# A decoder layer with expert retrieval on one core: the gate table read one chunk later, one gather of V rows per chunk of U, two list rows in the output tile, list places by fewer sums

## The chip, the core and the metric

The kernel runs on one of the eight cores of a Trainium2 chip. The metric is the device time of one execution in microseconds (us). Five engines work side by side, each through its own queue in order: TensorE (PE in the profile, PEld for its weight loads), VectorE (DVE), ScalarE (ACT), GpSimd (POOL) and SyncE (SP). SP and POOL mostly issue transfers here; all transfers run on the core's 16 DMA engines. [...]

## What is computed

One layer of a decoder on 256 tokens of width 2048: attention of two kinds, attention into a memory, and then retrieval of experts (PEER), which takes the second half of the time. Only that last part is touched:

```python
s = jnp.einsum('thpd,hpkd->thpk', q, sub_keys)          # 8 heads, 2 x 128 keys
top_s, top_i = lax.top_k(s, 16)
cand = top_s[:, :, 0, :, None] + top_s[:, :, 1, None, :]
best_s, best_c = lax.top_k(cand.reshape(T, 8, 256), 16)
expert = ia * 128 + ib                                   # one of 16384
gate = jax.nn.softmax(best_s, axis=-1)
...
a = jnp.einsum('td,ted->te', xb, u_tab[eb])
hidden = gb * jax.nn.gelu(a)
out = jnp.einsum('te,ted->td', hidden, v_tab[eb])
...
y = rmsnorm(h + out)
```

So each of the 256 tokens picks 8 x 16 experts; each expert is one row of U and one of V, 2048 numbers each.

## The kernel before, in words

Products are made in float32 by splitting: a raw tile of 128x1024 is loaded (SP, line 68), ACT rounds it to `hi` (line 77), DVE makes `lo` = raw - hi (line 79), and PE multiplies both parts (lines 133 and 135). There are four `raw` buffers, three `hi` and three `lo`.

**The U stretch.** All 16384 rows of U are multiplied with all 256 tokens, in 128 chunks of 128 experts. One chunk is two raw tiles, 1 MB in all. Its result lands in one of 16 tiles `hb` (eight chunks each; the first eight tiles lie in pool `ba`, the rest in `bb`), where GELU is applied. For the gates, 256 indirect transfers (`put_gate`, line 1119) scatter the gate numbers into a table in DRAM, three or four per chunk, until chunk 66. The table is then read back, four chunks' worth per transfer: for chunks 0 to 79 into a tile `gates` out of the `raw` buffers, one read per chunk of U from chunk `end` (68) on, and DVE multiplies it into `hb` (line 841) a chunk later; for chunks 80 to 127 straight into `hb` ahead of the chunk.

**The lists.** `counts` notes for each expert how many tokens of each half (0 to 127, 128 to 255) use it. `lists` then gives each expert a place in one of five lists: one token of half 0, one token of half 1, few tokens of half 0, few of half 1, and everything else. Part 0 covers chunks 0 to 83, part 1 chunks 84 to 127. The steps `flags`, `totals`, `ranks`, `offsets`, `place` and `spots` (lines 929 to 990) are some 40 small DVE instructions and a few PE ones, and their last product is `where`, the places. After that POOL writes one indirect transfer per chunk (line 996): 84 for part 0 during the U stretch, 44 for part 1 during the V stretch.

**The V stretch.** The lists are cut into 88 sets of 128 experts, ordered in bundles by `plan`. For each set POOL gathers 128 rows of V (`fetch`, line 1173, 1 MB) into a freed `hb` tile, and SP loads the set's hidden numbers (`begin`, line 1222, 128 KB, the tile `listed`, a `raw` buffer). A `few` or `all` set needs `hh` and `hl` of its list rows (lines 1209 and 1211) and three products per half of the row, a `one` set two. The bundles 0 to 4 hold six sets that concern tokens 0 to 127 alone. They run while the seven steps of part 1's lists stand between them on DVE and PE. Ten sets are gathered ahead: one per chunk of U from the moment part 0's writes are all issued, and two per chunk at chunks 123 and 124 (`behind` ties each to the `lo` of a half chunk). From the V stretch on, gathers run 12 and later 16 sets ahead, and every second half set POOL issues one of part 1's 44 writes between them.

The order of instructions on each engine is made by a list scheduler from the program text; waits follow from the tiles that instructions read and write.

`fin`, the 128 x 4 x 2048 output tile, takes the space of the pair tile that the products of U read; its last quarter `fin[:, 3]` is first written when the first half of the output is normalised, at the end.

Of the kernel before, what the change touches and what calls it, by code (L numbers as in the profile page):

```python
# [18 lines left out]
F32 = mybir.dt.float32  # L19
F32R = mybir.dt.float32r  # L20
U32 = mybir.dt.uint32
# [4 lines left out]
ALU = mybir.AluOpType  # L26
# [27 lines left out]
class Layer:  # L54
# [663 lines left out]
    def peer(self):  # L718
        nc, tc, a = self.nc, self.tc, self.a
        with ExitStack() as es:  # L720
# [3 lines left out]
            self.total = [ba.tile([128, 128], F32, name="total%d" % tb) for tb in range(2)]  # L724
            self.place = [ba.tile([128, 128], U32, name="place%d" % tb) for tb in range(2)]
# [28 lines left out]
            with ExitStack() as e2:  # L754
# [66 lines left out]
                early = list(range(0, first, 4))  # L821
                done = {}
                part = 0
                late, steps = [], []
                while c < 128:
# [23 lines left out]
                    for k in range(2 if c > 123 else 1):  # L849
                        if part == 1 and not late and len(self.sets) < 10:  # L850
                            self.fetch(len(self.sets))
                            self.behind(self.gather, 2 - k)
# [4 lines left out]
                assert part == 1 and len(self.sets) == 10 and not late and not puts, (c, late, self.sets)  # L857
# [53 lines left out]
    def lists(self, part, pool, tag, bufs):  # L911
# [13 lines left out]
        q, m = self.total[0][:, :n], self.total[1][:, :n]  # L925
# [35 lines left out]
        def offsets():  # L961
            room = self.rooms[:, part * 4:part * 4 + 4]
            rest, spot = small[:, 0:4], small[:, 4:9]
            self.pin(v.tensor_add(rest, got["sum"][:, :4], room))
            v.tensor_copy(spot[:, 0:1], got["sum"][:, 4:5])
            v.tensor_scalar_max(rest, rest, 0.0)
            for j in range(4):
                v.tensor_add(spot[:, j + 1:j + 2], spot[:, j:j + 1], rest[:, j:j + 1])
            v.tensor_scalar(self.over[:, part:part + 1], spot[:, 4:5], -limit, 0.0, op0=ALU.add, op1=ALU.max)
            self.hold = v.tensor_add(spot[:, :4], spot[:, :4], room)  # L970

        def place():
            p = got["p"]
            self.pin(v.tensor_mul(q, p[:, 4, :], f[:, 4]))
            for j in range(4):
                v.scalar_tensor_tensor(ok[:, j], p[:, j, :], float(cap[j] * 128), f[:, j], op0=ALU.is_lt, op1=ALU.mult)
            v.tensor_sub(f[:, :4], f[:, :4], ok)
            for j in range(4):
                v.scalar_tensor_tensor(m, p[:, j, :], small[:, 4 + j:5 + j], f[:, j], op0=ALU.add, op1=ALU.mult)
                v.tensor_add(q, q, m)  # L980
            v.tensor_reduce(out=m, in_=f.rearrange("p k e -> p e k"), axis=AX.X, op=ALU.add)
            for j in range(4):
                self.hold = v.scalar_tensor_tensor(ok[:, j], p[:, j, :], float(base[j] - BIG), ok[:, j], op0=ALU.add, op1=ALU.mult)

        def spots():
# [3 lines left out]
            v.tensor_reduce(out=q, in_=ok.rearrange("p k e -> p e k"), axis=AX.X, op=ALU.add)  # L989
            self.hold = v.scalar_tensor_tensor(where, q, float(BIG), x, op0=ALU.add, op1=ALU.add)  # L990
# [188 lines left out]
    def v_phase(self):  # L1179
# [6 lines left out]
        with ExitStack() as es:  # L1186
# [67 lines left out]
            def run(upto, beside=[], steps=[], every=2):  # L1254


                while at[0] < self.ends[upto]:
# [8 lines left out]
                    for hf in range(2):  # L1266
                        for unit in units:
# [5 lines left out]
                            if turn[0] % every:  # L1273
                                continue
                            if steps:
                                steps.pop(0)()
                            elif beside:
# [250 lines left out]
```

## Time and profile before

| what | value |
|---|---|
| three runs | 1677.89, 1681.62, 1684.51 us (median 1681.62) |
| the profiled execution | 1684.47 us, of which the span 1682.7 |
| TensorE busy | 1620.0 us (96%), 8760 matmuls |
| VectorE, ScalarE, GpSimd busy | 75%, 60%, 44% of the span |
| moved | 418.82 MB, 249 GB/s over the span |
| U stretch | to about 1361 us; V stretch after it |

A window row gives, for a stretch of time, the busy us of each engine with the number of its instructions in brackets, then the granted TensorE clock (1.00 is full), the mean busy share of the 16 DMA engines and the GB/s moved. A timeline row gives start, duration, engine, line, operation, tiles, count, and in square brackets how long the engine stood idle before it and whom it waited for. Since TensorE's busy time is modelled, the number of matmuls in a window says more than its busy share: with nothing late, some 58 to 59 of the U stretch's fall into 10 us.

### The profile page before, as it was taken

How to read it: one execution, taken by the hardware profiler on the slowest of the kernel's cores; microseconds unless marked ns; L12 is line 12 of the kernel's file. 1: busy time of each engine (PE TensorE's matmuls, PEld its weight loads, DVE VectorE, ACT ScalarE, POOL GpSimd, SP SyncE). 2: the span in 40 equal slices, each digit the busy share in tenths (PEclk: the TensorE clock that was granted, in tenths of full speed). 3: DMA queues.
4: the chain of work that ended last, by engine and by line, in shares of the span. 5: the costliest groups of instructions: out<-in, count | busy, mean ns of one | idle time of the engine just before them, and what ended most of it. 6: DMA issues, size and time to landing. Idle time of an engine off the chain costs nothing. (4 is left out here: it accounts for less than half of the span.)

```text
span 1682.7 us, 25655 instructions
## 1 busy us (share of the span) xinstructions
PE 1620.0 (96%) x8760; PEld 1376.6 (82%) x8760; DVE 1262.5 (75%) x2265; ACT 1001.5 (60%) x1486; POOL 748.3 (44%) x656
## 2 busy tenths in 40 slices
PE   8999999999999999999999999999999979989996
PEld 6878777888889888888888878878888858767884
DVE  6876575555668998999999648878665578868687
ACT  6645556775566656666656436665555457656576
POOL 5420000211305266667788761102776318887630
PEclk9999999999999999999999999999999999999998
DMA  8768435789956756666656648876998958998991
GB/s 291 240 200 285 132 119 180 285 319 355 353 179 217 254 178 188 181 188 187 184 178 191 192 150 278 301 258 226 276 271 260 366 191 337 393 372 307 420 411 65
DMA packets 119884, 418.82 MB, mean 249 GB/s; under 512 B 22713, under 2 KB 34633, under 8 KB 106048
## 3 DMA queue, kind: packets, MB, share of 16 engines
q1 hardware_dynamic: 79632, 252.41, 46.5%
q0 software_dynamic: 39824, 164.16, 26.4%
q8 instruction: 70, 1.15, 0.3%
q14 instruction: 70, 0.57, 0.1%
q10 hardware_dynamic: 288, 0.52, 0.1%
HBM read 373.16 MB, written 51.75 MB: 253 GB/s over the span
## 5 line engine op out<-in xcount | busy, mean ns | idle before, releaser
L79 DVE TENSOR_TENSOR lo<-raw,hi 128x1024 fp32r<-128x1024 f32 x437 | 541.2, 1243 | 210.7 <-ACT hi L77 189.5
L77 ACT ACTIVATE hi<-raw 128x1024 fp32r<-128x1024 f32 x437 | 459.4, 1055 | 358.9 <-issue 145.7
L133 PE MATMUL acc<-pair_f,hi 128*128 128x512 f32 x2288 | 576.8, 394 | 6.1 <-ACT hi L77 6.1
L133 PEld LDWEIGHTS acc<-pair_f,hi 128*128 128x128 f32 x2288 | 412.4, 189 | 82.1 <-ACT hi L77 7.9
L1119 POOL DMA_INDIRECT table<-total,place x256 | 312.0, 1219 | 139.7 <-DVE lo L79 63.3
L135 PEld LDWEIGHTS acc<-pair_f,lo 128*128 128x128 f32 x2288 | 311.6, 191 | 30.8 <-DVE lo L79 9.3
L135 PE MATMUL acc<-pair_f,lo 128*128 128x256 f32 x2288 | 320.3, 283 | 7.0 <-DVE lo L79 7.0
L996 POOL DMA_INDIRECT rows<-hb,where x128 | 155.8, 1217 | 47.2 <-issue 28.9
L1173 POOL DMA_INDIRECT vrows<-V,index x88 | 125.9, 1430 | 112.2 <-issue 38.4
L115 DVE SCALAR_TENSOR_TENSOR lo<-vrows,val,hi 128x1024 fp32r<-128x1024 f32 x96 | 122.3, 1281 | 44.6 <-ACT hi L113 35.8
L113 ACT ACTIVATE hi<-vrows,val 128x1024 fp32r<-128x1024 f32 x96 | 108.6, 1146 | 74.4 <-PE out L1202 26.6
L133 PE MATMUL acc<-pair_x,hi 128*128 128x512 f32 x512 | 131.6, 395 | 2.0 <-ACT hi L77 2.0
L133 PEld LDWEIGHTS acc<-pair_x,hi 128*128 128x128 f32 x512 | 91.3, 189 | 18.8 <-ACT hi L77 2.4
L79 DVE TENSOR_TENSOR lo<-vrows,hi 128x1024 fp32r<-128x1024 f32 x80 | 97.3, 1219 | 8.7 <-PE out L1202 3.1
L77 ACT ACTIVATE hi<-vrows 128x1024 fp32r<-128x1024 f32 x80 | 84.0, 1052 | 24.2 <-PE out L1202 13.9
L1202 PE MATMUL out<-hi,hh 128*128 128x512 f32 x256 | 79.9, 406 | 2.3 <-ACT hi L77 1.5
L1202 PE MATMUL out<-hi,hl 128*128 128x512 f32 x256 | 81.1, 402 | 0.8 <-DVE hl L1211 0.5
L1202 PE MATMUL out<-lo,hh 128*128 128x512 f32 x256 | 75.2, 397 | 6.1 <-DVE lo L79 5.9
L135 PEld LDWEIGHTS acc<-pair_x,lo 128*128 128x128 f32 x512 | 70.1, 190 | 7.8 <-DVE lo L79 3.0
L135 PE MATMUL acc<-pair_x,lo 128*128 128x256 f32 x512 | 74.7, 285 | 1.8 <-DVE lo L79 1.7
L133 PE MATMUL acc<-pair_o,hi 128*128 128x512 f32 x256 | 65.2, 394 | 2.4 <-ACT hi L77 1.4
L1202 PE MATMUL out<-hi,listed 128*128 128x512 f32 x192 | 58.0, 398 | 7.5 <-ACT hi L113 7.4
(401 smaller groups left out, 2182.6 us busy)
## 6 DMA issues: line engine op xcount, KB each, us to landing
raw<-U SPq DMA_DIRECT2D x256, 512.0 KB, 4.3
raw<-w_sb SPq DMA_DIRECT2D x32, 512.0 KB, 4.5
table<-zero POOLq DMA_DIRECT2D x16, 1024.0 KB
raw<-w_out SPq DMA_DIRECT2D x32, 512.0 KB, 6.7
raw<-w_pq SPq DMA_DIRECT2D x32, 512.0 KB, 4.3
listed<-rows SPq DMA_DIRECT2D x88, 128.0 KB, 7.5
rows<-zero POOLq DMA_DIRECT2D x12, 903.0 KB
gates<-table POOLq DMA_DIRECT2D x20, 512.0 KB
```

The source lines that it names most:

```text
L77: self.last_hi = nc.scalar.activation(hi, raw, AF.Copy)
L79: self.last_lo = (eng or nc.vector).tensor_tensor(out=lo, in0=raw, in1=hi.bitcast(F32), op=ALU.subtract)
L113: nc.scalar.activation(hi, raw, AF.Copy, scale=val)
L115: self.last_lo = nc.vector.scalar_tensor_tensor(lo, raw, val, hi.bitcast(F32), op0=ALU.mult, op1=ALU.subtract)
L133: mm(ps, hi[:, n * m:(n + 1) * m], pair[:, k, :], start=first and n == 0, stop=False)
L135: self.last_mm = mm(ps[:, T:], lo[:, n * m:(n + 1) * m], pair[:, k, :T], start=False, stop=last and n == len(ks) - 1)
L996: ins = nc.gpsimd.indirect_dma_start(out=self.rows[part], out_offset=bass.IndirectOffsetOnAxis(ap=where[:, i - lo:i - lo + 1], axis=0), in ...
L1119: ins = self.nc.gpsimd.indirect_dma_start(out=self.table, out_offset=bass.IndirectOffsetOnAxis(ap=self.place[tb][:, s:s + 1], axis=0), in_ ...
L1173: self.gather = nc.gpsimd.indirect_dma_start(out=raw, out_offset=None, in_=self.a["V"], in_offset=bass.IndirectOffsetOnAxis(ap=self.index[ ...
L1202: self.last_mm = mm(out[tb][hf * 2 + q], h, v[:, q * 512:(q + 1) * 512], start=first and n == 0, stop=last and n == len(passes) - 1)
```

## The change

The table's read for chunks 0 to 79 starts at chunk 69 instead of 68 (`end += 1` after `first` was worked out from the old value). V rows are gathered one set per chunk, and none after chunk 126; what is missing to ten is gathered behind the last half chunk of U. The list rows of bundles 2 and 3 go into `fin[:, 3]` instead of a `raw` buffer. `place` and `spots` write the terms of a sum side by side into one tile and add them with one reduction, where they added them one after another; for that, `total` and `place` become four parts of one tile of 128x512. The last edit, in `run`, is the same loop written otherwise: no instruction moves by it.

```diff
-            self.total = [ba.tile([128, 128], F32, name="total%d" % tb) for tb in range(2)]
-            self.place = [ba.tile([128, 128], U32, name="place%d" % tb) for tb in range(2)]
+            self.spare = ba.tile([128, 512], F32, name="totals")
+            self.total = [self.spare[:, tb * 128:(tb + 1) * 128] for tb in range(2)]
+            self.place = [self.spare[:, (tb + 2) * 128:(tb + 3) * 128].bitcast(U32) for tb in range(2)]
...
                 early = list(range(0, first, 4))
+                end += 1
...
-                    for k in range(2 if c > 123 else 1):
-                        if part == 1 and not late and len(self.sets) < 10:
-                            self.fetch(len(self.sets))
-                            self.behind(self.gather, 2 - k)
+                    if part == 1 and not late and c < 127:
+                        self.fetch(len(self.sets))
+                        self.behind(self.gather, 2)
...
+                while len(self.sets) < 10:
+                    self.fetch(len(self.sets))
+                    self.behind(self.gather, 1)
...
-        q, m = self.total[0][:, :n], self.total[1][:, :n]
+        t5 = self.spare[:, :5 * n].rearrange("p (k e) -> p k e", k=5)
+        m = self.spare[:, 5 * n:6 * n]
...
-            self.hold = v.tensor_add(spot[:, :4], spot[:, :4], room)
+            self.hold = v.scalar_tensor_tensor(spot[:, :4], spot[:, :4], float(base[ALL] - BIG), room, op0=ALU.add, op1=ALU.add)
...
         def place():
             p = got["p"]
-            self.pin(v.tensor_mul(q, p[:, 4, :], f[:, 4]))
             for j in range(4):
-                v.scalar_tensor_tensor(ok[:, j], p[:, j, :], float(cap[j] * 128), f[:, j], op0=ALU.is_lt, op1=ALU.mult)
+                ins = v.scalar_tensor_tensor(ok[:, j], p[:, j, :], float(cap[j] * 128), f[:, j], op0=ALU.is_lt, op1=ALU.mult)
+                if j == 0:
+                    self.pin(ins)
+            v.scalar_tensor_tensor(t5[:, 4], p[:, 4, :], float(base[ALL] - BIG), f[:, 4], op0=ALU.add, op1=ALU.mult)
             v.tensor_sub(f[:, :4], f[:, :4], ok)
             for j in range(4):
-                v.scalar_tensor_tensor(m, p[:, j, :], small[:, 4 + j:5 + j], f[:, j], op0=ALU.add, op1=ALU.mult)
-                v.tensor_add(q, q, m)
-            v.tensor_reduce(out=m, in_=f.rearrange("p k e -> p e k"), axis=AX.X, op=ALU.add)
+                v.scalar_tensor_tensor(ok[:, j], p[:, j, :], float(base[j] - BIG), ok[:, j], op0=ALU.add, op1=ALU.mult)
             for j in range(4):
-                self.hold = v.scalar_tensor_tensor(ok[:, j], p[:, j, :], float(base[j] - BIG), ok[:, j], op0=ALU.add, op1=ALU.mult)
+                self.hold = v.scalar_tensor_tensor(t5[:, j], p[:, j, :], small[:, 4 + j:5 + j], f[:, j], op0=ALU.add, op1=ALU.mult)

         def spots():
-            self.pin(v.tensor_scalar(x, q, limit, ROWS[part] - limit - base[ALL], op0=ALU.is_ge, op1=ALU.mult))
-            v.scalar_tensor_tensor(x, q, float(base[ALL] - BIG), x, op0=ALU.add, op1=ALU.add)
-            v.tensor_mul(x, x, m)
-            v.tensor_reduce(out=q, in_=ok.rearrange("p k e -> p e k"), axis=AX.X, op=ALU.add)
-            self.hold = v.scalar_tensor_tensor(where, q, float(BIG), x, op0=ALU.add, op1=ALU.add)
+            self.pin(v.tensor_reduce(out=x, in_=t5.rearrange("p k e -> p e k"), axis=AX.X, op=ALU.add))
+            v.tensor_reduce(out=m, in_=f.rearrange("p k e -> p e k"), axis=AX.X, op=ALU.add)
+            v.tensor_reduce(out=t5[:, 0], in_=ok.rearrange("p k e -> p e k"), axis=AX.X, op=ALU.add)
+            v.scalar_tensor_tensor(m, x, limit + base[ALL] - BIG, m, op0=ALU.is_ge, op1=ALU.mult)
+            v.scalar_tensor_tensor(t5[:, 1], x, float(BIG), t5[:, 0], op0=ALU.add, op1=ALU.add)
+            self.hold = v.scalar_tensor_tensor(where, m, ROWS[part] - limit - base[ALL], t5[:, 1], op0=ALU.mult, op1=ALU.add)
...
-                t = self.st.tile([128, HALF], F32, tag="raw", name="listed", bufs=RAW)
+                if at[0] in (2, 3):
+                    t = fin[:, 3, (at[0] - 2) * HALF:(at[0] - 1) * HALF]
+                else:
+                    t = self.st.tile([128, HALF], F32, tag="raw", name="listed", bufs=RAW)
```

Since a scheduler sets the order, the rows themselves show what moved. On DVE, at the end of chunk 65's work, the first product with the read table (`hb<-hb,gates`) stood before and stands now:

```order
L169 TENSOR_TENSOR hb<-hb,acc 128x256
L841 TENSOR_TENSOR hb<-hb,gates 128x4x256
L79 TENSOR_TENSOR lo<-raw,hi 128x1024
L907 TENSOR_REDUCE count<-signs 128x2x2 x2
L79 TENSOR_TENSOR lo<-raw,hi 128x1024
```

```order
L169 TENSOR_TENSOR hb<-hb,acc 128x256
L79 TENSOR_TENSOR lo<-raw,hi 128x1024
L843 TENSOR_TENSOR hb<-hb,gates 128x4x256
L79 TENSOR_TENSOR lo<-raw,hi 128x1024
L169 TENSOR_TENSOR hb<-hb,acc 128x256
L911 TENSOR_REDUCE count<-signs 128x2x2 x2
```

The first is before, the second the change. The product has moved behind one `lo`, that is behind half a chunk, not a whole one: the scheduler puts it where its model sees room.

On SP, the list rows of part 0 (`rows_80`) for the first sets, before and now (`flag_i` is a flag that is loaded between them):

```order
L68 DMA raw<-U 128x1024 x256
L1222 DMA listed<-rows_80 128x256 x13
L1397 TENSOR_LOAD flag_i
L1397 ISA x2
L1222 DMA listed<-rows_80 128x256 x44
```

```order
L68 DMA raw<-U 128x1024 x256
L1231 DMA listed<-rows_80 128x256 x6
L1231 DMA fin<-rows_80 128x256 x2
L1231 DMA listed<-rows_80 128x256 x5
L1404 TENSOR_LOAD flag_i
L1404 ISA x2
L1231 DMA listed<-rows_80 128x256 x44
```

The four `raw` buffers now go to bundles 0, 1, 4 and 5 (six sets), whose rows are loaded first; the rows of bundles 2 and 3 come after them and wait until PE has read the pair tile for the last time.

On DVE, part 1's `place` and `spots` (`f` the flags, `ps_rank` the ranks in PSUM), from the first of `place` on, before:

```order
L979 SCALAR_TENSOR_TENSOR total_4915<-ps_rank,small,f 128x44
L980 TENSOR_TENSOR total_4914<-total_4914,total_4915 128x44
L1211 TENSOR_TENSOR hl<-listed,hh 128x256
L1230 TENSOR_SCALAR listed<-listed 128x128
...
L979 SCALAR_TENSOR_TENSOR total_4915<-ps_rank,small,f 128x44
L983 SCALAR_TENSOR_TENSOR ok<-ps_rank,ok 128x44 x4
L980 TENSOR_TENSOR total_4914<-total_4914,total_4915 128x44
L79 TENSOR_TENSOR lo<-vrows,hi 128x1024
L981 TENSOR_REDUCE total_4915<-f 128x44
```

and now:

```order
L986 SCALAR_TENSOR_TENSOR ok<-ps_rank,ok 128x44 x4
L988 SCALAR_TENSOR_TENSOR totals<-ps_rank,small,f 128x44 x4
L79 TENSOR_TENSOR lo<-vrows,hi 128x1024
L992 TENSOR_REDUCE totals<-f 128x44
L1217 TENSOR_TENSOR hl<-listed,hh 128x256
L991 TENSOR_REDUCE x<-totals 128x44
L993 TENSOR_REDUCE totals<-ok 128x44
L994 SCALAR_TENSOR_TENSOR totals<-x,totals 128x44
L995 SCALAR_TENSOR_TENSOR totals<-x,totals 128x44
L996 SCALAR_TENSOR_TENSOR where<-totals 128x44
```

The four pairs of product and sum that took turns have become four products in a row and one reduction over five terms.

More of the change, by code (lines that the diff above doesn't have):

```diff
@@ L856, in peer @@
                         some(late, 0)
-                assert part == 1 and len(self.sets) == 10 and not late and not puts, (c, late, self.sets)
+                assert part == 1 and 5 < len(self.sets) < 10 and not late and not puts, (c, late, self.sets)
+                while len(self.sets) < 10:
+                    self.fetch(len(self.sets))
+                    self.behind(self.gather, 1)
             self.accs.close()
@@ L977, in place @@
+            v.scalar_tensor_tensor(t5[:, 4], p[:, 4, :], float(base[ALL] - BIG), f[:, 4], op0=ALU.add, op1=ALU.mult)
             v.tensor_sub(f[:, :4], f[:, :4], ok)
             for j in range(4):
-                v.scalar_tensor_tensor(m, p[:, j, :], small[:, 4 + j:5 + j], f[:, j], op0=ALU.add, op1=ALU.mult)
-                v.tensor_add(q, q, m)
-            v.tensor_reduce(out=m, in_=f.rearrange("p k e -> p e k"), axis=AX.X, op=ALU.add)
-            for j in range(4):
-                self.hold = v.scalar_tensor_tensor(ok[:, j], p[:, j, :], float(base[j] - BIG), ok[:, j], op0=ALU.add, op1=ALU.mult)
@@ L985, in spots @@
-        def spots():
-            self.pin(v.tensor_scalar(x, q, limit, ROWS[part] - limit - base[ALL], op0=ALU.is_ge, op1=ALU.mult))
-            v.scalar_tensor_tensor(x, q, float(base[ALL] - BIG), x, op0=ALU.add, op1=ALU.add)
-            v.tensor_mul(x, x, m)
-            v.tensor_reduce(out=q, in_=ok.rearrange("p k e -> p e k"), axis=AX.X, op=ALU.add)
-            self.hold = v.scalar_tensor_tensor(where, q, float(BIG), x, op0=ALU.add, op1=ALU.add)
+                v.scalar_tensor_tensor(ok[:, j], p[:, j, :], float(base[j] - BIG), ok[:, j], op0=ALU.add, op1=ALU.mult)
@@ new lines, in place, with spots @@
+            for j in range(4):
+                self.hold = v.scalar_tensor_tensor(t5[:, j], p[:, j, :], small[:, 4 + j:5 + j], f[:, j], op0=ALU.add, op1=ALU.mult)
+        def spots():
+            self.pin(v.tensor_reduce(out=x, in_=t5.rearrange("p k e -> p e k"), axis=AX.X, op=ALU.add))
+            v.tensor_reduce(out=m, in_=f.rearrange("p k e -> p e k"), axis=AX.X, op=ALU.add)
+            v.tensor_reduce(out=t5[:, 0], in_=ok.rearrange("p k e -> p e k"), axis=AX.X, op=ALU.add)
+            v.scalar_tensor_tensor(m, x, limit + base[ALL] - BIG, m, op0=ALU.is_ge, op1=ALU.mult)
+            v.scalar_tensor_tensor(t5[:, 1], x, float(BIG), t5[:, 0], op0=ALU.add, op1=ALU.add)
+            self.hold = v.scalar_tensor_tensor(where, m, ROWS[part] - limit - base[ALL], t5[:, 1], op0=ALU.mult, op1=ALU.add)
@@ L1272, in run @@
                                 continue
-                            if turn[0] % every:
-                                continue
-                            if steps:
+                            if every == 1 and steps:
                                 steps.pop(0)()
-                            elif beside:
+                            if every == 2 and turn[0] % 2 == 0 and beside:
                                 ins = beside.pop(0)()
```

## The prediction

> **What bounds the kernel now.** I read the page first, then windows of 10 us, then the timeline wherever a window fell short. The page:
>
> ```profile
> PE 1620.0 (96%) x8760; PEld 1376.6 (82%) x8760; DVE 1262.5 (75%) x2265; ACT 1001.5 (60%) x1486; POOL 748.3 (44%) x656
> ```
>
> TensorE has work nearly all the time, so only a place where it waits can pay, and what it pays is read there. The windows find the places:
>
> ```profile
> 1000.00:1010.00 10.00, 6.32 (x36) 5.30 (x35) 3.43 (x4) 2.11 (x4) 1.15 (x2) 0.97 0.24 61
> 1010.00:1020.00 10.00, 10.00 (x53) 8.71 (x52) 9.04 (x12) 6.48 (x12) 1.06 (x2) 0.85 0.86 304
> ...
> 1320.00:1330.00 10.00, 10.00 (x59) 8.82 (x59) 5.02 (x7) 3.99 (x7) 1.98 (x2) 1.00 1.01 335
> 1330.00:1340.00 10.00, 8.40 (x47) 6.91 (x46) 3.98 (x6) 4.13 (x6) 3.03 (x3) 1.00 1.02 392
> 1340.00:1350.00 10.00, 8.12 (x44) 6.70 (x43) 6.58 (x11) 4.74 (x9) 1.00 (x1) 1.00 1.02 425
> 1350.00:1360.00 10.00, 8.67 (x48) 7.25 (x47) 6.35 (x9) 6.50 (x10) 0.00 (x0) 1.00 0.27 90
> 1360.00:1370.00 10.00, 8.83 (x47) 6.09 (x45) 8.00 (x21) 7.21 (x12) 1.99 (x2) 1.00 0.38 100
> 1370.00:1380.00 10.00, 6.46 (x31) 4.56 (x30) 7.53 (x29) 4.42 (x6) 2.34 (x2) 1.00 0.91 344
> 1380.00:1390.00 10.00, 5.58 (x14) 3.31 (x15) 9.50 (x25) 3.65 (x4) 4.25 (x3) 0.75 0.34 116
> 1395.00:1520.00 125.00, 115.83 (x477) 91.49 (x477) 98.64 (x125) 81.07 (x87) 103.16 (x73) 0.96 1.00 386
> 1570.00:1580.00 10.00, 10.00 (x46) 8.28 (x45) 6.32 (x7) 7.19 (x8) 5.22 (x6) 1.00 1.02 422
> ```
>
> Four things are to be seen. At 1000 to 1010 TensorE starves while the transfer engines idle (24%). At 1330 to 1350 it starves while they are full. At the start of V it starves with VectorE at 9.5 of 10, and the transfers idle again. From 1395 to 1520 the transfers are full (1.00), GpSimd is busy 103 of 125 us, and TensorE gets 477 matmuls where the V stretch fits 46 into 10 us when nothing is late (last row): this stretch ends when its transfers have been issued and moved, not when TensorE likes.
>
> **The table read a chunk later.** The timeline at the first stall:
>
> ```profile
> 995.31 1.22 DVE L79 TENSOR_TENSOR lo<-raw,hi 128x1024 fp32r<-128x1024 f32 x1 [1.57 <-ACT hi L77]
> 997.01 1.06 ACT L77 ACTIVATE hi<-raw 128x1024 fp32r<-128x1024 f32 x1 [1.46 <-issue]
> 1002.83 0.58 POOL L881 DMA_DIRECT2D gates<-table  x1 [4.16 <-issue]
> 1003.30 2.00 PE L133 MATMUL acc<-pair_f,hi 128*128 128x512 f32 x8
> 1006.57 1.23 DVE L841 TENSOR_TENSOR hb<-hb,gates 128x1024 f32<-128x1024 f32 x1 [9.71 <-DMA gates<-table]
> 1007.71 1.22 DVE L79 TENSOR_TENSOR lo<-raw,hi 128x1024 fp32r<-128x1024 f32 x1
> 1008.99 1.69 PE L135 MATMUL acc<-pair_f,lo 128*128 128x256 f32 x8 [3.68 <-DVE lo L79]
> 1010.48 3.13 PE L133 MATMUL acc<-pair_f,hi 128*128 128x512 f32 x8
> 1014.40 2.00 PE L133 MATMUL acc<-pair_f,hi 128*128 128x512 f32 x8
> 1017.20 2.00 PE L133 MATMUL acc<-pair_f,hi 128*128 128x512 f32 x8
> ```
>
> The first product waits 9.71 us for a table that can't be read before the last scatter lands; the next `lo` stands behind it. A half chunk takes 2.80 us (1014.40 to 1017.20). From 1003.30 to 1010.48 one took 7.18, and the next 3.92 with its first group at 3.13 instead of 2.00: 4.4 + 1.1 = 5.5 us lost, the last part to the clock (0.85 granted).
>
> In the new order one `lo` goes ahead of the product: its `hi` is there at 998.1, so it is ready at about 999.3. The read keeps its time (the scatters set it), so the product still ends at 1007.7 and the `lo` behind it at 1008.9; TensorE, half a chunk further, wants that one at 1008.1: 0.9 us late. The second read no longer takes the first one's buffer but that of this `lo`, so it is issued at about 1009.2; landing 3.7 us later as the first did, its product ends at 1014.1 and the `lo` behind that at 1015.3, wanted at 1014.6 or before: another 0.7 to 1.2. Left are 2.1 of 5.5: **3.4 us gained**, between 0.5 (the second wait takes the place of the first) and 5.
>
> [...]
>
> All that hangs on the read moves a chunk: part 0's lists and its 84 writes end a chunk later, which costs only V sets, below. TensorE's smaller stalls at 1105 to 1140 depend on which reads meet; I take 0 for them, between -2.5 and +2.5.
>
> **One gather per chunk.**
>
> ```profile
> 1325.86 1.04 POOL L1173 DMA_INDIRECT vrows<-V,index  x1 [6.38 <-DVE lo L79]
> 1328.93 2.00 PE L133 MATMUL acc<-pair_f,hi 128*128 128x512 f32 x8
> 1330.02 1.02 POOL L1173 DMA_INDIRECT vrows<-V,index  x1 [2.19 <-DVE lo L79]
> 1331.47 1.06 ACT L77 ACTIVATE hi<-raw 128x1024 fp32r<-128x1024 f32 x1 [2.46 <-DMA raw<-U]
> 1341.06 1.00 POOL L1173 DMA_INDIRECT vrows<-V,index  x1 [1.73 <-DVE lo L79]
> 1357.85 2.11 PE L133 MATMUL acc<-pair_f,hi 128*128 128x512 f32 x8 [0.51 <-ACT hi L77]
> ```
>
> From 1325.86 to 1341.06 five gathers come, one per 3.8 us, U's raw tiles land late, ACT waits for them and TensorE for ACT. From 1328.93 to 1357.85 eight half chunks take 28.9 us instead of 22.4: 6.5 lost. One gather of 1.05 MB beside 1.05 MB of U per 5.6 us asks for 375 GB/s; the windows show 335 with 59 matmuls and no loss, and 392 to 425 with loss. So I leave 0.5: **6.0 us gained**, bounds 3.5 and 6.5. Seven sets are gathered by U's end instead of ten, since the first chunk that may gather is now 119 and the last 125.
>
> **The three sets behind U** are issued with U's last `lo`, when the transfers were 27% and 38% busy (1350 to 1370); 3.15 MB at 386 GB/s take 8.1 us. TensorE reaches the eighth set after bundles 0 to 4 and one more (over 68 matmuls, 15 us). Taken as 0, up to 8.1 if they push later transfers back.
>
> **The lists' places.** The V stretch's full part begins when `where` is ready:
>
> ```profile
> 1359.80 1.11 PE L135 MATMUL acc<-pair_f,lo 128*128 128x256 f32 x8
> 1364.53 0.17 DVE L936 TENSOR_SCALAR f<-f 128x44 bf16<-128x44 bf16 x1
> 1376.55 0.29 DVE L1228 TENSOR_REDUCE val<-listed 128x1 f32<-128x128 f32 x1 [2.29 <-DMA listed<-rows]
> 1378.88 0.73 PE L1202 MATMUL out<-lo,hh 128*128 128x512 f32 x2 [2.68 <-DVE lo L79]
> 1379.79 0.26 DVE L979 SCALAR_TENSOR_TENSOR total<-ps_rank,small,f 128x44 f32<-128x44 f32 x1
> 1382.33 0.52 DVE L983 SCALAR_TENSOR_TENSOR ok<-ps_rank,ok 128x44 f32<-128x44 f32 x4
> 1385.09 0.46 DVE L989 TENSOR_REDUCE total<-ok 128x44 f32<-128x176 f32 x1
> 1386.08 1.80 POOL L996 DMA_INDIRECT rows<-hb,where  x1 [5.45 <-DVE where L990]
> ```
>
> Three pieces. The wait of 2.29 for a list row in the middle of `offsets` goes: that row is loaded before U ends now. Products and sums taking turns last from 1379.79 to 1382.85, 3.1 us with 0.66 of list work in between; eight products side by side pass at 0.13 each (0.52 for four), 1.05: 1.4 to 1.9 saved. `spots` gains a reduction of 220 elements (0.46 for 176, so some 0.57) and drops two operations: 0.4 lost. Together **3.8 us**; 0 if the rows in `fin`, which can't be loaded before TensorE's last product of U, make VectorE wait as long, 5 if the dropped waits let TensorE keep its clock (0.75 at 1380). Why this reaches the end, from GpSimd's waits between 1390 and 1530 (us in all, times, longest) and the list loads:
>
> ```profile
> POOL rows L996 <- issue: 8.5, 28, 0.3
> POOL vrows L1173 <- issue: 8.4, 27, 0.5
> DMA to landing us min/median/max: 2.0/7.5/12.9
> ```
>
> From 1390 to 1530 GpSimd waits for nothing longer than 0.5 us, so its 44 writes and the gathers between them start earlier by what `where` does, and the U stretch's gain passes through. U's last product ends at 1360.9 (1359.80 and 1.11). The flags are done 3.8 us after it (1364.53), and five `lo` of 1.2 and a cast stand between them and VectorE's first use of a row in `fin`: some 10 us after U's end, where lists land in 7.5 at the median (last row).
>
> [...]
>
> The merged tile adds no wait on any engine, and the loop in `run` is the same: 0.
>
> **The sum.** 3.4 + 6.0 + 3.8 = 13.2 us. From the profiled execution's 1684.47 that gives 1671.3; it stands 2.85 above the median of the runs, 1681.62, so the forecast is **1668.5**.
>
> **The rivals.**
> - *The places come no earlier*: the `fin` rows land among three gathers and VectorE waits there instead. For it the median of 7.5 and maximum of 12.9 in busy stretches, against it the 10 us. 3.8 less: 1672.2.
> - *The first stall only moves*: VectorE is 90% busy at 1010 to 1020, while the table is read, and the second product waits as the first did. 0.5 instead of 3.4: 1671.4.
> - *Only U's end pays*, the change not doing what it says in the other two places: 6.0, so 1675.6.
> - *The three sets come out of V's budget*: if the transfers from U's end on are the bound, 8.1 us come back: 1676.6. Against it 27% and 38% at 1350 to 1370.
> - *Slower: list rows at the back of the queue.* If the two loads into `fin` are served only after the gathers around U's end, five of 1.05 MB at 386 GB/s (13.6 us) and then 12.9, they land 26.5 us after U; VectorE stands from 10 on, `where` and all of V slip 16.3, and the clock falls (1.1 as after the first stall, twice). It decides from 10 + 13.2 = 23 us on: 1668.5 + 16.3 + 2 = 1687. Against it: the longest landing of 88 is 12.9.
>
> [...]
>
> **How the numbers follow.** Chances: the forecast 0.50, places no earlier 0.17, stall moved 0.08, only U's end 0.12, V's budget 0.08, slower 0.05. A measurement here tells 0.5% from no change, 8.4 us: faster means under 1673.2. Of the forecast 0.46 lies there, of the next two (close to the edge) 0.16 together: 0.62. The rest up to 1690 holds 0.33; above it 0.05 for the slower rival and what the new order does elsewhere. The range goes from 1661, all upper bounds at once with the stalls at 1105 (5 + 6.5 + 5 + 2.5 = 19) and the runs' own spread, to 1680, past the budget rival; the forecast's own is 1664 to 1673.
>
> **What would show it.** One wait of about 1 us before L135 near 1008 and none of 3; matmuls at 58 to 59 per 10 us through U's last 30 us, with seven gathers in them; the first write of part 1 about 21 us after U's last product instead of 25; the same 134 us from there to where TensorE's windows are full again. Wrong would be: a VectorE wait for `fin` rows above 1 us, raw tiles of U still late, or TensorE idle after U for want of V rows.

## The result, and the profile after

| | before | after |
|---|---|---|
| median of six runs each | 1682.06 us (1677.89 to 1684.51) | 1672.32 us (1669.49 to 1676.29) |
| ratio, 95% interval | | 0.9941 [0.9924, 0.9957] |
| the profiled execution's span | 1682.7 us | 1674.5 us |

The change gains 9.9 us (7.2 to 12.8 by the interval). The forecast was 13.2. Total and sign are right, so the question is whether the three sums behind them are. The page after:

```profile
PE 1617.0 (97%) x8760; PEld 1374.8 (82%) x8760; DVE 1261.1 (75%) x2257; ACT 1000.9 (60%) x1486; POOL 746.5 (45%) x656
```

Its windows, with the columns as before:

```profile
1000.00:1010.00 10.00, 10.00 (x60) 8.84 (x59) 4.94 (x7) 4.36 (x7) 1.16 (x2) 1.00 0.50 161
1010.00:1020.00 10.00, 9.69 (x55) 8.16 (x54) 7.14 (x9) 5.60 (x10) 0.53 (x1) 1.00 0.72 218
...
1030.00:1040.00 10.00, 7.95 (x46) 7.00 (x47) 9.40 (x12) 7.06 (x11) 1.06 (x2) 1.00 0.67 215
1120.00:1130.00 10.00, 7.28 (x42) 6.18 (x43) 8.43 (x13) 5.96 (x11) 0.76 (x1) 1.00 0.84 309
1330.00:1340.00 10.00, 10.00 (x59) 8.79 (x58) 4.61 (x8) 3.73 (x6) 3.01 (x3) 1.00 0.99 345
1340.00:1350.00 10.00, 9.15 (x50) 7.57 (x49) 6.79 (x9) 5.37 (x9) 0.00 (x0) 1.00 0.75 296
1350.00:1360.00 10.00, 7.11 (x39) 6.12 (x38) 5.90 (x14) 6.62 (x12) 4.07 (x3) 0.95 0.53 168
```

Before, 1000 to 1010 held 36 matmuls; now it holds 60. But 1030 to 1040, which held 60, now holds 46. The row before the change:

```profile
1030.00:1040.00 10.00, 10.00 (x60) 8.88 (x59) 9.53 (x12) 7.06 (x11) 1.06 (x2) 1.00 0.76 251
```

At U's end the hole of 1330 to 1350 (47 and 44 matmuls) is nearly closed, and the first window of V has a new one.

To say how much, the program is cut at the same places in every profile: the start of TensorE's first group (line 133) of chunks 62, 95, 116 and 127, then the first write of part 1, then the end of the span. Before, those four groups are

```profile
972.58 2.00 PE L133 MATMUL acc<-pair_f,hi 128*128 128x512 f32 x8
...
1168.75 1.09 PE L133 MATMUL acc<-pair_f,hi 128*128 128x512 f32 x4
...
1287.03 0.86 PE L133 MATMUL acc<-pair_f,hi 128*128 128x512 f32 x3
...
1354.39 0.86 PE L133 MATMUL acc<-pair_f,hi 128*128 128x512 f32 x3
```

and after

```profile
973.83 2.00 PE L133 MATMUL acc<-pair_f,hi 128*128 128x512 f32 x8
...
1170.01 0.86 PE L133 MATMUL acc<-pair_f,hi 128*128 128x512 f32 x3
...
1287.33 0.63 PE L133 MATMUL acc<-pair_f,hi 128*128 128x512 f32 x2
...
1350.37 0.86 PE L133 MATMUL acc<-pair_f,hi 128*128 128x512 f32 x3
```

(In some, the first matmuls of a group are listed in a row of their own; a row's start is what counts.) A chunk with nothing late takes 5.59 us, two half chunks of 2.79.

| stretch | nothing late | before | after | gain | forecast |
|---|---|---|---|---|---|
| chunks 62 to 94, where the table is read | 184.4 | 196.17 | 196.18 | 0.0 | 3.4 |
| chunks 95 to 115 | 117.3 | 118.28 | 117.32 | 1.0 | 0 |
| chunks 116 to 126, U's end | 61.5 | 67.36 | 63.04 | 4.3 | 6.0, with the next row |
| chunk 127 to the first write of part 1 | | 31.69 | 29.01 | 2.7 | 3.8 for the lists |
| first write of part 1 to the end | | 296.62 | 295.12 | 1.5 | 0 |

That makes 9.5; the start of the program took 1.3 us longer, so 8.2 are left between the two spans. The waits at the table, after:

```profile
1000.61 0.58 POOL L885 DMA_DIRECT2D gates<-table  x1 [1.96 <-DVE lo L79]
1005.64 1.23 DVE L843 TENSOR_TENSOR hb<-hb,gates 128x1024 f32<-128x1024 f32 x1 [5.06 <-DMA gates<-table]
...
1015.25 1.22 PE L135 MATMUL acc<-pair_f,lo 128*128 128x256 f32 x8 [0.31 <-DVE lo L79]
...
1021.63 0.53 POOL L885 DMA_DIRECT2D gates<-table  x1 [5.62 <-DVE hb L843]
...
1029.63 1.23 DVE L843 TENSOR_TENSOR hb<-hb,gates 128x1024 f32<-128x1024 f32 x1 [4.17 <-DMA gates<-table]
...
1032.05 1.22 PE L135 MATMUL acc<-pair_f,lo 128*128 128x256 f32 x8 [2.46 <-DVE lo L79]
```

The first wait went further than forecast: from 3.68 to nothing, then 0.31 behind the second read. Then the fourth read, issued at 1021.63, is there at 1029.63, 8.0 us later; its neighbours take 3.8 to 5.9. VectorE stands 4.17 us in front of the product, the `lo` behind it is late, TensorE waits 2.46. The place forecast for a wait (near 1008) has none, and the loss is elsewhere.

V's start after:

```profile
1356.34 0.29 DVE L1237 TENSOR_REDUCE val<-listed 128x1 f32<-128x128 f32 x1 [0.84 <-DMA listed<-rows]
...
1357.45 1.04 ACT L77 ACTIVATE hi<-vrows 128x1024 fp32r<-128x1024 f32 x1
...
1358.40 0.36 ACT L168 ACTIVATE ut<-acc 128x256 f32<-128x256 f32 x1
...
1359.01 2.08 PE L1208 MATMUL out<-hi,hh 128*128 128x512 f32 x4 [2.89 <-ACT hh L1215]
...
1361.06 0.20 DVE L936 TENSOR_TENSOR f<-count 128x44 bf16<-128x44 f32 x1
...
1374.92 0.77 DVE L988 SCALAR_TENSOR_TENSOR totals<-ps_rank,small,f 128x44 f32<-128x44 f32 x4
...
1377.57 0.56 DVE L991 TENSOR_REDUCE x<-totals 128x44 f32<-128x220 f32 x1
...
1378.89 0.20 DVE L996 SCALAR_TENSOR_TENSOR where<-totals 128x44 uint32<-128x44 f32 x1
1379.38 1.81 POOL L1002 DMA_INDIRECT rows<-hb,where  x1 [4.04 <-DVE where L996]
```

U's last product ends at 1356.12, the flags of part 1 begin at 1361.06, 4.9 us later; before it was 2.7 (1360.91 to 1363.63). A list row that is not there yet (0.84) and a split of V rows stand in front of the last join of U, on VectorE and ScalarE, and TensorE waits 2.89 for `hh`. From the flags to the first write it takes 18.3 us where it took 22.4. So the lists gained 4.1, and 2.2 of that went before they began. The first write comes 23.3 us after U's last product, where it was 25.2.

### The profile page after: what moved, and what is told of

Read it like the earlier page. It is cut to its first block, busy times and chain, and to the rows that moved or that the text cites. A ratio compares the mean times of both kernels' runs of the same rounds, so it can differ in the third digit from the quotient of the medians.

```text
span 1674.5 us, 25643 instructions
## 1 busy us (share of the span) xinstructions
PE 1617.0 (97%) x8760; PEld 1374.8 (82%) x8760; DVE 1261.1 (75%) x2257; ACT 1000.9 (60%) x1486; POOL 746.5 (45%) x656
## 5 line engine op out<-in xcount | busy, mean ns | idle before, releaser
L1125 POOL DMA_INDIRECT table<-totals x256 | 311.7, 1218 | 138.5 <-DVE lo L79 62.7
L135 PEld LDWEIGHTS acc<-pair_f,lo 128*128 128x128 f32 x2288 | 311.0, 190 | 30.3 <-DVE lo L79 8.7
L1002 POOL DMA_INDIRECT rows<-hb,where x128 | 159.5, 1246 | 52.2 <-issue 30.4
L1179 POOL DMA_INDIRECT vrows<-V,index x88 | 120.3, 1367 | 101.8 <-issue 23.2
L133 PEld LDWEIGHTS acc<-pair_x,hi 128*128 128x128 f32 x512 | 91.4, 189 | 18.4 <-ACT hi L77 2.0
L133 PE MATMUL acc<-pair_o,hi 128*128 128x512 f32 x256 | 65.2, 394 | 2.4 <-ACT hi L77 1.4
```

Of the source, the lines that this page charges most:

```text
L133: mm(ps, hi[:, n * m:(n + 1) * m], pair[:, k, :], start=first and n == 0, stop=False)
L135: self.last_mm = mm(ps[:, T:], lo[:, n * m:(n + 1) * m], pair[:, k, :T], start=False, stop=last and n == len(ks) - 1)
L1002: ins = nc.gpsimd.indirect_dma_start(out=self.rows[part], out_offset=bass.IndirectOffsetOnAxis(ap=where[:, i - lo:i - lo + 1], axis=0), in ...
L1125: ins = self.nc.gpsimd.indirect_dma_start(out=self.table, out_offset=bass.IndirectOffsetOnAxis(ap=self.place[tb][:, s:s + 1], axis=0), in_ ...
L1179: self.gather = nc.gpsimd.indirect_dma_start(out=raw, out_offset=None, in_=self.a["V"], in_offset=bass.IndirectOffsetOnAxis(ap=self.index[ ...
```

## The experiments

The theory after this reading: the wait at the table is moved, not removed; the slower gather pace pays at U's end and costs at the start of V; rows in `fin` and fewer sums are worth what was forecast. The rivals: each part is worth its forecast by itself; a part does nothing; a later stretch swallows what an earlier one gives. Each part was undone alone, then done alone, and the disputed cause of the table's waits was taken away. The chips differ: on two of the four the kernel before took 1696.45 and 1689.74, so every ratio is to the kernel before on the same chip, and times in us are the ratio's difference times 1682. The stretches are from one profile of each run. On the two slower chips GpSimd takes 130 to 133 us for part 0's 84 writes, on the other two 124 to 127, and the kernel before has a profile on one chip alone; so a stretch is compared across chips with care.

### Each part undone

```diff
 k1_end_undone
-                end += 1
 k2_pace_undone
-                    if part == 1 and not late and c < 127:
-                        self.fetch(len(self.sets))
-                        self.behind(self.gather, 2)
+                    for k in range(2 if c > 123 else 1):
+                        if part == 1 and not late and len(self.sets) < 10:
+                            self.fetch(len(self.sets))
+                            self.behind(self.gather, 2 - k)
...
-                while len(self.sets) < 10:
-                    self.fetch(len(self.sets))
-                    self.behind(self.gather, 1)
 k3_fin_undone
-                if at[0] in (2, 3):
-                    t = fin[:, 3, (at[0] - 2) * HALF:(at[0] - 1) * HALF]
-                else:
-                    t = self.st.tile([128, HALF], F32, tag="raw", name="listed", bufs=RAW)
+                t = self.st.tile([128, HALF], F32, tag="raw", name="listed", bufs=RAW)
 k4_sums_undone: place, spots, total and place as they were before the change
```

> The changed kernel with the table read from chunk 68 on again; all else as changed. Theory 'the reading stretch gives it back': the first wait of 9.7 us for the table and TensorE's loss of 5.5 us near 1003 to 1014 return, but the losses that the changed kernel shows at 1030 to 1040 and in part at 1100 to 1130 (some 4.4 us) go, so the time is 1.2 us above the changed kernel's 1672.3: 1673.5, and the twenty reads' last product ends about 1 us later than the changed kernel's 1123.1 + 1.2, not 5. The prediction's reading (nothing is given back): 1675.7, 3.4 above. Rival 'the reads keep their order and it is the first wait alone': 1677.8, 5.5 above.

> The changed kernel with ten sets gathered before U ends and two per chunk from chunk 124 on. Theory 'starved U hid its own epilogue': U's last product comes 4.9 us later, but the last joins of chunks 126 and 127 are then done as soon as U ends, so the flags come 2.7 us after U's last product instead of 4.9, and the first write of part 1 some 21 us after it: 2.7 us above the changed kernel, 1675.0. Rival 'the parts add up': 4.9 above, 1677.2. Rival 'the three sets behind U cost transfers in V' (the transfers are the bound from there on): 0 or below, 1672.3 or less.

> The changed kernel with the list rows of bundles 2 and 3 in raw buffers again. Prediction's reading: VectorE waits about 2.3 us for a list row in the middle of the offsets again, and the first write of part 1 moves by that: 1674.6. Rival 'the wait was there only because U's end was starved, or it falls elsewhere': the wait is under 0.5 us and the time within 0.5 of 1672.3. Rival 'rows in fin are the late ones': below 1672.

> The changed kernel with place and spots summed one after another again (and total and place as tiles of their own). Prediction's reading: the chain from the first product of place to where is 1.0 to 1.5 us longer, so the first write of part 1 and the end come that much later: 1673.3 to 1673.8. Rival 'VectorE fills the gaps of the chain with lo work that is wanted anyway': where comes 1.5 later and the end does not: 1672.3, within 0.5.

| run | ratio to before | chunks 62 to 94 | U's end | flags after U | flags to write |
|---|---|---|---|---|---|
| the change | 0.9941 [0.9924, 0.9957] | 196.18 | 63.04 | 4.94 | 18.32 |
| read from chunk 68 again | 0.9955 [0.9933, 0.9976] | 197.07 | 64.98 | 3.08 | 18.43 |
| old gather pace | 0.9922 [0.9891, 0.9953] | 195.98 | 63.68 | 3.30 | 18.80 |
| list rows in `raw` again | 0.9952 [0.9930, 0.9975] | 195.82 | 64.44 | 4.49 | 19.79 |
| old sums | 0.9963 [0.9941, 0.9985] | 191.08 | 63.43 | 5.37 | 20.00 |

No ratio is clearly apart from the change's, so the stretches have to speak. Reading from chunk 68 again costs 2.4 us, with 2 gained to 7 lost left open, so none of its three expected times is excluded. Three things follow from the stretches. With the old pace U's end takes 63.7, not 67.4: once the gathers start at chunk 120, doubling them does not make the loss, and the expectation that U's end would come 4.9 later is wrong. The lists' two halves both show: from flags to write 1.5 us for the rows in `fin`, 1.7 for the sums, where kernels that have both halves lie within 0.5 of each other (18.3 to 18.8). And the stretch of the table took 191.08 in a kernel whose table reads are those of the change: 5 us of it change from one profile to another.

### The change again, the read alone, and reads that need no raw buffer

```diff
 b1_end_only: the kernel before with
+                end += 1
 c1_gates_own: the change with
-                        t = self.st.tile([128, HALF], F32, tag="raw", name="gates", bufs=RAW)
-                        t = t[:, :4 * T].rearrange("p (i t) -> p i t", t=T)
-                        self.table_read(t, g)
+                        k = g // 4 % 4
+                        t = self.buf[14 + k // 2][:, k % 2 * 4:k % 2 * 4 + 4, :T]
+                        self.behind(self.table_read(t, g), 1)
 c2_gates_own_end: c1_gates_own and
-                end += 1
...
-                        done.setdefault(c + 1, []).append((g, t))
+                        done.setdefault(c + 2, []).append((g, t))
```

> The changed kernel once more, as a measure of how much of its trace repeats. In the first profile TensorE took 198.97 us for the 33 chunks 62 to 94, as much as before the change, with one half chunk of 5.51 at chunk 72 where a table read took 8.0 us to land. Theory 'that landing was chance': here 194 to 195, as where the sums alone were undone (193.87). Rival 'the reading stretch gives back what the first wait gained': 198.5 to 199 again. The time stands 0.59% under the kernel before within 0.2 in both.

> The changed kernel with the table reads for chunks 0 to 79 going to four places in the tiles of chunks 112 to 127, which are empty until then, instead of a raw buffer; each read is still multiplied in a chunk later and issued behind the last lo of the chunk before. Theory 'TensorE loses 9 us at chunks 84 to 94 because a read that waits for the product before it lands late and lo stands behind its product': reads can now be issued 5 us earlier, the waits of VectorE for the table go below 0.3 us, chunks 62 to 94 take 184 to 188 us instead of 194 to 199, and the time falls by about 8 us against the changed kernel. Rival 'VectorE is the bound there' (lo 2.46, join 0.42, product 1.23, counts 1.27 of 5.59 us a chunk): 1 to 3 us. Rival 'the transfers are' (U 1.05 MB and the table 0.52 to 1.05 MB a chunk): chunks 84 to 94 still take 69.

> The same four places, the table read from chunk 68 on as before the change, and each read multiplied in two chunks later instead of one, so that the lists end with the chunk where the changed kernel's do. Theory as for the run with one chunk: no wait of VectorE for the table at all, chunks 62 to 94 in 184 to 186 us, the time 10 us under the changed kernel. Rival 'VectorE is the bound': as much as the run with one chunk, within 2 us.

> The kernel before with the first part of the change alone: the table read from chunk 69 on. Prediction's reading: 3.4 us under the kernel before and U's end as it was (TensorE's half chunks from chunk 116 to 127 in 67.4 us). Rival 'the later start spares U's end': the ten gathers begin at chunk 120 and end at 126, chunks 116 to 126 take 63.7 us as in the changed kernel with the old pace, so 3.7 us are gained there and the reading stretch gives 0 to 5 more: 4 to 9 us under. Rival 'nothing': the stall moves and U's end stays, within 1 us of the kernel before.

| run | median | ratio to before | chunks 62 to 94 | U's end | flags after U |
|---|---|---|---|---|---|
| the change again | 1673.23 us | 0.9944 [0.9923, 0.9964] | 194.87 | 63.68 | 4.90 |
| four places of their own | 1669.19 us | 0.9925 [0.9904, 0.9946] | 192.24 | 64.36 | 4.80 |
| the same, a chunk more to land | 1668.32 us | 0.9918 [0.9898, 0.9937] | 189.08 | 65.16 | 4.94 |
| before, read a chunk later | 1679.18 us | 0.9978 [0.9964, 0.9992] | 196.46 | 62.83 | 3.09 |

The change repeats to 0.0003, and its stretch of the table is 1.3 us shorter: 194.87. The 198.97 and 193.87 that the expectation compares with start half a chunk (2.79) too early; counted as in these tables they are 196.18 and 191.08, so 194.87 lies between its theory and its rival. The same read, in the change again:

```profile
1021.74 0.53 POOL L885 DMA_DIRECT2D gates<-table  x1 [5.33 <-DVE hb L843]
1027.30 1.23 DVE L843 TENSOR_TENSOR hb<-hb,gates 128x1024 f32<-128x1024 f32 x1 [1.62 <-DMA gates<-table]
```

It lands in 5.6 us instead of 8.0, VectorE's wait is 1.62, and TensorE loses nothing there. So that one landing was chance, as the first theory of the expectation has it. The stretch gains little by it, since other half chunks lose more: the first of chunk 88 takes 5.39 where it took 3.86.

The read a chunk later, alone, gains 3.7 us (1.3 to 6.1), about what was forecast for it, and none of it shows where it was forecast: its stretch takes 196.46 (196.17 before), and U's end 62.83 instead of 67.36. The gathers give a reading of that. With the read moved alone, GpSimd's first, eighth and last gather and the last raw tiles of U:

```profile
1313.44 1.07 POOL L1174 DMA_INDIRECT vrows<-V,index  x1 [5.05 <-DMA index<-rows]
...
1341.12 1.01 POOL L1174 DMA_INDIRECT vrows<-V,index  x1 [4.16 <-DVE lo L79]
...
1346.80 1.00 POOL L1174 DMA_INDIRECT vrows<-V,index  x1 [0.30 <-DVE hb L898]
...
1349.87 1.06 ACT L77 ACTIVATE hi<-raw 128x1024 fp32r<-128x1024 f32 x1 [2.36 <-DMA raw<-U]
1350.98 2.11 PE L133 MATMUL acc<-pair_f,hi 128*128 128x512 f32 x8 [1.60 <-ACT hi L77]
```

Ten gathers run here too, at the old pace, and the raw tiles are late too (2.36). But the first gather comes in chunk 120 instead of 118, and the first half chunk longer than 2.9 us is that of chunk 126, with three half chunks behind it. In all fourteen profiles that first long half chunk comes 4.5 to 5.5 chunks after the first gather, whatever the pace. In the change ScalarE's first wait for a raw tile behind the first gather (1311.10) ends at 1323.30 (1.80), 12.2 us after it, and the first long half chunk begins at 1340.50; that the tiles loaded ahead last for the time between is the author's reading and was not shown. U's end by the chunk of the first gather:

| first gather in chunk | U's end, two per chunk at the end | U's end, one per chunk |
|---|---|---|
| 118.5 to 119 | 67.36 (before) | 64.98 |
| 119.5 | | 64.40 |
| 120 | 64.22, 63.68 | 63.04, 63.68, 64.36, 65.16 |
| 120.5 to 121 | 64.24, 62.83, 62.26 | 64.44, 63.43 |

Only in the first row do the paces differ clearly, and there the starts differ too (118.5 and 119). From chunk 119 on the values lie between 62.3 and 65.2 in little order, so the table shows that the one start before 119 has the long end, and no more. And it is not the read alone that moves the start. The kernel with only the lists changed (64.22) and the one with only the pace changed (64.40) read from chunk 68 and start at 120 and 119.5: on their chip GpSimd took 132.9 and 130.0 us for part 0's writes, 124.0 in the kernel before. A later start through the read fits the first write of part 0, which is issued 5.0 us later in the change (1174.07 after 1169.04); that this shortens U's end rests on one profile of the kernel before.

Places of their own for the table's reads take 2.6 and 5.8 us off the stretch against the change again. That misses both expectations: the waits of VectorE for the table do not go below 0.3. With a chunk to land, chunks 84 to 94, where the theory put the loss, still take 69.3 (67.9 and 68.3 in the change), as the rival "the transfers are" has it, and the 2.6 lie in the range of the rival "VectorE is the bound"; what bounds the stretch was not settled. VectorE's and TensorE's waits from 1000 to 1130, in us, times, longest, in the change

```profile
PE acc L135 <- DVE lo L79: 5.3, 6, 2.5
DVE hb L843 <- DMA gates<-table: 25.8, 19, 5.1
```

and with four places and a chunk more to land

```profile
PE acc L135 <- DVE lo L79: 1.6, 3, 0.7
DVE hb L842 <- DMA hb<-table: 19.0, 14, 3.5
```

VectorE still waits 19.0, fewer times and as long each time (1.4 us on average in both), but TensorE waits for `lo` only 1.6 instead of 5.3. Both kernels were the fastest of their chip, 4 to 5 us under the change by the medians of six. The intervals of the ratios overlap, so the order is likely, not certain. The second has the lowest ratio of the study, 0.9918, though other kernels lie within its interval.

### The other parts alone, and the pace once more

```diff
 b2_pace_only: the kernel before with the new lines of the gathers
 b3_lists_only: the kernel before with the rows in fin and the new place and spots
 k5_pace_undone_again: as k2_pace_undone
 c4_gates_own_old_pace: c2_gates_own_end with the old lines of the gathers
```

> The kernel before with the second part of the change alone: one gather per chunk, none after chunk 126, the missing sets behind U's last half chunk. Prediction's reading (doubled gathers starve U's end): 6.0 us under the kernel before, 8 half chunks at the end of U regular to within 0.5. Rival 'the chunk in which the gathers start is what counts, not their pace': at the old start chunks 116 to 126 take 65.0 us (as where the read's chunk alone was undone) instead of 67.4, 2.4 gained, and the flags of part 1's lists come 3 to 5 us after U's last product instead of 2.7: 0 to 2 us under.

> The kernel before with the last two parts alone: list rows of bundles 2 and 3 in the output tile, and the places by fewer sums. Prediction's reading: the first write of part 1 comes 21 us after U's last product instead of 25.2, and V's end follows: 3.8 us under the kernel before. Rival 'V's transfers are the bound': the first write moves by 4 and the end by less than 1.

> The changed kernel with the old gather pace (ten sets before U ends, two per chunk from 124 on), the run of before repeated beside the single parts. Prediction's reading (the pace is worth 6.0): 6 us above the changed kernel's 0.9942 of the kernel before, so 0.9978. Rival 'once the gathers start at chunk 120 the pace buys nothing, and the late sets cost the epilogue': chunks 116 to 126 in 63 to 64 us as with the new pace, the flags 3.2 us after U's last product instead of 4.9, so 0 to 2 us below the changed kernel: 0.993 to 0.994.

> The kernel with the table read into four empty places from chunk 68 on and multiplied in two chunks later (0.9918 of the kernel before), with the old gather pace. By the rival of the run before (the pace buys nothing): flags 1.7 us earlier after U's end, U's end not longer, so 1 to 3 us lower, 0.990 to 0.991. By the prediction's reading: U's end starves again, 6 us higher, 0.995.

| run | ratio to before | chunks 62 to 94 | U's end | flags after U | flags to write |
|---|---|---|---|---|---|
| before, new pace | 1.0005 [0.9980, 1.0029] | 188.25 | 64.40 | 3.58 | 23.97 |
| before, rows in `fin` and new sums | 0.9962 [0.9940, 0.9984] | 193.37 | 64.22 | 3.65 | 18.38 |
| the change, old pace | 0.9955 [0.9933, 0.9978] | 188.47 | 64.24 | 3.30 | 18.81 |
| four places, old pace | 0.9922 [0.9896, 0.9948] | 188.17 | 62.26 | 4.76 | 18.82 |

The pace alone is worth nothing that can be measured (3 us gained to 5 lost are left open). The change without it, two times on two chips, is 0.9922 and 0.9955, on both sides of the change's 0.9941 and 0.9944. The lists alone gain 6.4 us (2.7 to 10.1), and their 18.4 from flags to write is the same as in the change; the rival that V's transfers swallow it, the end moving by less than 1, falls. The three parts alone add up to 0.55% [-0.22, +0.05, -0.38], the whole to 0.59%: within intervals of 0.14 to 0.25 each, no loss between them shows.

Taking the old pace with the four places (0.9922) gives no more than the new pace with them (0.9918), so the expected 1 to 3 us did not come. The flags came late there too (4.76) although the pace is the old one, because VectorE waits 1.37 just ahead of them for a list row; without it they would come after 3.4, as with the old pace elsewhere (3.30). In the change the delay is in the order of the rows shown above, and that was seen again (0.80 for the list row, 2.85 before `hh`) in its second profile; why some of the kernels have the join of chunk 127 ahead was not tried.

The stretch of the table was 188.25 and 193.37 in two kernels that still read from chunk 68. Their first read finds TensorE further back: it is issued 23.7 and 25.5 us after the start of chunk 62, where before it was 30.3 (1002.83 and 972.58). In the kernel before, the last ten scatters ahead of it wait for no other engine; the last three are

```profile
994.90 0.98 POOL L1119 DMA_INDIRECT table<-total,place  x1 [0.30 <-issue]
996.18 1.20 POOL L1119 DMA_INDIRECT table<-total,place  x1 [0.30 <-issue]
997.69 0.98 POOL L1119 DMA_INDIRECT table<-total,place  x1 [0.31 <-issue]
```

one after the other with 0.30 between. How long the first product waits reads therefore as a race between GpSimd's 256 scatters and TensorE's chunks. Where TensorE lost some 9 us earlier (half chunks of 3.4 to 5.4 at chunks 57 to 59 in both), the stall of 5.5 is not there to be gained.

## Why the prediction was right, and where it was wrong

**The table read a chunk later (3.4 forecast).** The amount is right, 3.7 measured alone (1.3 to 6.1), but by luck; the step that failed is "Left are 2.1 of 5.5" with "I take 0" for the stalls at 1105 to 1140. The first stall went whole, but chunks 62 to 94 did not get shorter: 196.18 and 194.87 with the change and 196.46 with the read alone, against 196.17 before (188.25, 193.37 and 197.07 in the kernels on the slower chips that read from 68). The rival "the first stall only moves" has this stretch. In the profiles the gain lies at U's end, at a step that the prediction dismissed in one sentence ("All that hangs on the read moves a chunk: ... which costs only V sets"): the writes of part 0 end later, the gathers start 1.5 to 2 chunks later, and fewer half chunks of U are left when the first long one comes. That this is where the 3.7 come from is likely, not shown: the long end stands in one profile, and kernels that read from chunk 68 also started late on another chip.

**One gather per chunk (6.0 forecast).** U's end gained 4.3, but not by this. The step that failed is the reading of the rows from 1325.86 to 1341.06, "five gathers come, one per 3.8 us, U's raw tiles land late", as a loss that the doubled pace makes: the tiles are late with seven gathers or ten (2.36 above with ten and no loss before chunk 126). Counted over the prediction's own eight half chunks, 6.5 us were lost before; with the new pace 1.6 to 4.1 are lost, with the old pace and a start at chunk 120 or later 1.9 to 3.9. So 375 GB/s against 392 to 425 does not decide; when the gathers start does, as far as the profiles go. The pace alone measures 1.0005. Raw tiles of U still late, one of the prediction's signs of being wrong, came true with the change itself: ScalarE waits up to 3.16 for one at 1327.82.

**The three sets behind U (0 forecast).** From the first write to the end the profiles run from 290.8 to 298.5 us, with ten sets gathered before U's end as with fewer, so no price of 8.1 shows; one smaller than that spread can't be told.

**The lists' places (3.8 forecast).** From flags to write 4.1 us were gained; undone one at a time, the rows in `fin` were worth 1.5 and the sums 1.7. The four products took 0.77 against 0.52 forecast, the new reduction of 220 elements 0.56 against 0.57. No wait of VectorE for rows in `fin` stands in the profile, so the rivals "the places come no earlier" and "list rows at the back of the queue" fall. The mis-sized term is the start: "the flags are done 3.8 us after" U's last product, which became 2.2 more (4.9 instead of 2.7 to their first row), because a list row and a V split now stand ahead of U's last join. Hence 1.9 from U's last product to the first write, not 3.8. (In the slower rival the slip is 26.5 - 10 = 16.5, not 16.3, which changes nothing.)

**What carries through.** From the first write to the end 295.1 against 296.6: the gain of U and the lists passes through, as forecast, though the 1.5 between them is small beside the 290.8 to 298.5 of all profiles.

The forecast gain was 3.3 too high. Part by part, 3.4 + 6.0 + 3.8 stand against 3.7 - 0.8 + 6.4 measured alone, each measured to 2 to 4 us either way. So one term is right in size and wrong in place, one is nothing, and the last came out larger, with 3.8 inside its interval. Errors in opposite directions made the sum look better than its steps, and that is luck.

## What to carry to other kernels

A part that delays one thing may pay where something else was colliding: follow everything that hangs on the delayed event to the end, and ask what each then no longer meets. Before a part gets the credit, look whether kernels without it show the same: here two kernels without the later read had the shorter end of U too. Before a loss is put down to a rate, look when it begins and count how much work is left from there. And do each part alone before its name is put on a gain: here the change's total was right, and the part with the largest forecast did nothing.

## What the runs showed of the hardware

**In the profiles of the kernel before and of the change the stretches of half clock begin on a grid of 3.413 us, and three of them come after a window with 1.44 to 1.53 us of matmul in it.** Before the change they begin at 1009.50, 1384.96, 1463.47, 1501.02, 1514.67 and 1671.68, with it at 1358.98, 1379.46, 1495.51 and 1662.76, in each profile whole multiples of 3.413 apart. The one at 1358.98 begins just as TensorE resumes after 2.89 us. Two pairs of windows on that grid, after:

```profile
1355.57:1358.98 3.41, 0.55 (x5) 0.34 (x3) 1.36 (x5) 2.21 (x5) 2.47 (x3) 1.00 0.72 220
1358.98:1362.39 3.41, 3.38 (x8) 2.75 (x9) 2.58 (x12) 1.44 (x4) 0.00 (x0) 0.50 1.03 410
1027.89:1031.30 3.41, 1.70 (x8) 1.06 (x6) 1.67 (x2) 0.35 (x1) 0.15 (x1) 1.00 0.15 59
1031.30:1034.71 3.41, 2.66 (x15) 2.35 (x16) 3.34 (x5) 3.00 (x6) 0.38 (x1) 1.00 0.67 183
```

The second column is TensorE's, the last but two its granted clock. A window with 0.55 us of matmul is followed by one at 0.50; one with 1.70 is followed by full clock here, the wait of 2.46 from 1029.59 to 1032.05 falling on both sides of its edge. Before the change, a window with 1.48 was followed by 1.00 and one with 1.50 by 0.50:

```profile
1374.72:1378.13 3.41, 1.48 (x7) 0.90 (x5) 1.55 (x9) 0.85 (x1) 0.00 (x0) 1.00 1.05 398
1378.13:1381.54 3.41, 1.93 (x6) 0.97 (x6) 3.12 (x15) 1.36 (x2) 1.02 (x1) 1.00 0.48 139
1460.06:1463.47 3.41, 1.50 (x6) 0.63 (x5) 1.25 (x2) 1.48 (x2) 2.56 (x3) 1.00 1.00 396
1463.47:1466.88 3.41, 3.41 (x9) 2.18 (x9) 3.31 (x3) 3.32 (x4) 3.04 (x2) 0.50 1.01 406
```

From 11 us on, the eight windows at full clock with 0.50 to 1.44 us of matmul in these two profiles are each followed by 0.50 (1.44 in the one from 1511.26, before), and all with 1.62 or more by 1.00 (1.62 in the one from 1488.68, after); between them, the one with 1.48 is followed by 1.00, those with 1.50 and 1.53 (1659.35, after) by 0.50. So busy time, which is modelled, gives no sharp edge. Of the two waits above, the 2.89 that lie almost wholly in one window were followed by 3.41 us at half clock, the 2.46 that lie in two by none.

**A table read of 0.52 MB took 3.8 to 8.0 us in the change from issue to its use, beside U's loads**, twenty reads in all. The same read differs from one execution to the next: the fourth took 8.0 us in the first profile of the change and 5.6 in the second. So a wait can be there in one execution and not in another: VectorE's for that read was 4.17 us and then 1.62, TensorE's behind it 2.46 and then none.

**One profile of a kernel is one throw.** Chunks 62 to 94 took 196.18 and 194.87 us in two executions of the change, and 195.98 and 188.47 in two of the change with the old pace, on two chips; the stretch from the first write on took 295.12 and 293.51 with the change. A ledger of a few microseconds needs the second profile, of the kernel before too.
